# Transformer trunk on one Trainium2 core: one pool for the two MLP products, two pairs of the wide layer kept in DRAM as both parts, the fourth bank's seed put ahead

## The chip, the cores and the metric

The kernel runs on one core of one Trainium2 chip. TensorE (PE) multiplies matrices into PSUM banks, VectorE (DVE) and ScalarE (ACT) move and combine tiles, and SyncE (SP) does nothing but issue DMAs, one after the other, on one queue that 16 DMA engines serve. The metric is the device time of one execution in microseconds (us); a smaller one is better. Times in the text are counted from the start of the profiled span.

## The reference

One layer of a hybrid trunk over 2048 tokens of width 1024, all float32. A normalised input is projected once; some columns go through a short gated convolution, others through a chunked state-space scan; one output projection joins them, then comes the MLP, on which most of the change lies, and a last normalisation:

```python
h = rmsnorm(x, norm_mix_w)
proj = h @ w_in                              # 1024 columns to 5648
y_a = u_b * causal_dwconv(u_c * u_h, conv_w)
y_b = rmsnorm(ssd_scan(silu(conv(xbc)), dt, ...) * silu(z), norm_w)
x = x + concat(y_a, y_b) @ w_out
h = rmsnorm(x, norm_mlp_w)
hid = square(relu(h @ w_up))                 # 2048 x 4096: the wide layer
x = x + hid @ w_down
return rmsnorm(x, final_norm_w)
```

## The kernel before

**Number format.** Every large product is computed from two parts: a tile is cast to the type fp32r (the part `hi`, on ScalarE), and VectorE subtracts that from the tile (the part `lo`). Three matmuls make one product, `hi·hi`, `hi·lo`, `lo·hi` (lines 276 to 278, all of 128x512). Weights are split in the same way (lines 100 and 101: `whi`, `wlo`).

**Seven products.** A block of the MLP is cut 2 by 2 and computed by seven products in place of eight: b11, t1, t2, b21, t3, b22, t4, in this order, on combined operands. They add into the PSUM tiles px, py and pw. Right after b11, ScalarE copies px into a bank of its own, pw (line 283, the "seed"), on which b21 goes on. `chain` is the function that issues the seven, and after each it calls the code that empties the banks.

**Stages.** The up product runs in two halves of the tokens, each over 16 pairs of column blocks, 84 matmuls a pair; its input lies in four "places" u0 to u3 in SBUF, each with two parts (`uh`, `ul`). The result of a pair, after relu and square, is combined to seven blocks and stored to DRAM (`hid_d`, line 861 for three stores of two blocks, 862 for the seventh). The down product then reads the pairs back: `refill` loads them into raw tiles `rh` (line 970), and `settle` splits these into the places with a cast on ScalarE (347) and a subtraction on VectorE (348), which need the places to be free of the up product. `STEPS` says what the down product does in turn: step 0 handles output block d=0 with pairs 0 to 3, step 1 block d=2 with pairs 0 and 1, and so on. VectorE adds each bank to an `acc` tile (line 1018) that was loaded with the residual (line 978). The turn from the up to the down product, at about 2000 us, is where all of this meets; the text calls it the turn.

**Order.** The code is recorded in program order with tile pools; a scheduler then places the instructions of each engine. A tile that takes over a buffer waits for whoever used it last. The up product's pool (tags `utmp`, 8 buffers, and `uhid`, 5) is closed before the down product's (tag `acc`, 18) opens in the same memory. SP issues DMAs in its order, and each of them waits for the DMA that stands eight places ahead of it on the queue, or thereabouts (eight counters are used in turn, `DMAHW0` to `DMAHW7`).

**The scan** runs beside the projections, in 32 chunks. In each, ScalarE computes decays (lines 1268 and 1269: eight relus, a table load and an exp on `dec`, which a DMA brought), and casts `xde` to `xtok` (line 1276) for the first matmul of the state (`st`, line 113).

Of the kernel before, what the change touches and what calls it, by code (L numbers as in the profile page):

```python
# [11 lines left out]
F32 = mybir.dt.float32  # L12
# [14 lines left out]
EPS = 1e-5  # L27
FF = 4096
# [11 lines left out]
def trunk(ctx: ExitStack, tc: tile.TileContext, x, w_in, w_dt, w_out, w_up, w_down, cvec, hrow, out):  # L40
# [24 lines left out]
    hid_d = [[dram.tile([P, 7, TB], F32, name=f"hid_d{h}_{q}") for q in range(NQ)] for h in range(2)]  # L65
    sums_d = {}
# [124 lines left out]
    class Seven:  # L191
# [19 lines left out]
        def sums(self, e0, e1, e2, t4):  # L211

            self.sub(e2[:, 0], e2[:, 1], e0[:, 1])
            self.sub(e0[:, 1], e0[:, 1], e0[:, 0])
            self.sub(e1[:, 0], e2[:, 1], e0[:, 1])
            self.sub(t4, e1[:, 1], e1[:, 0])

# [27 lines left out]
        def chain(self, groups, ws, ahead, evict, after):  # L245
# [18 lines left out]
            for name, wn, half, acc in PRODUCTS:  # L264
# [568 lines left out]
    class Mlp(Seven):  # L833
# [18 lines left out]
        def wide(self, name):  # L852
            return self.up.tile([P, 2, TB], F32, tag="uhid", name=name, bufs=5)

        def store(self, h, q, e0, e1, e2):
            t4 = self.tmp("t4")
            if h == 1 and q >= LAST:
                nc.sync.dma_start(b12_d[:, q - LAST], e0[:, 1])
            self.sums(e0, e1, e2, t4)
            for i, e in enumerate((e0, e1, e2)):  # L860
                nc.sync.dma_start(hid_d[h][q][:, 2 * i : 2 * i + 2], e)
            nc.sync.dma_start(hid_d[h][q][:, 6], t4)

        def pair(self, h, q, ws, ahead, after):

            e0, e1, e2 = (self.wide(n) for n in ("e0", "e1", "e2"))
            s = {}
# [5 lines left out]
            def add(o, pm, name):  # L873
                nc.vector.tensor_tensor(out=o, in0=pm, in1=s[name], op=ALU.add)
# [5 lines left out]
            def evict(name, gi, pm):  # L880
                if name == "b11":
                    if gi not in self.seeds:
                        copy(pm["x"], "s1")
                elif name == "t1":
                    copy(pm["y"], "s5")
                elif name == "t2":
                    copy(pm["x"], "s2")
                elif name == "b21":
                    if gi in self.seeds:
                        relu2(e0[:, 0], pm["w"])  # L890
                    else:
                        add(e0[:, 0], pm["w"], "s1")
                        relu2(e0[:, 0], e0[:, 0])
                elif name == "t3":
                    add(e2[:, 1], pm["x"], "s5")
                    relu2(e2[:, 1], e2[:, 1])
                elif name == "b22":
                    add(e0[:, 1], pm["y"], "s2")
                    relu2(e0[:, 1], e0[:, 1])
                else:  # L900
                    relu2(e1[:, 1], pm["x"])

            got = self.chain([self.places], ws, ahead, evict, after)
            self.store(h, q, e0, e1, e2)
# [54 lines left out]
        def refill(self, gs, name):  # L959

            i = {"t1": 0, "b21": 1, "b22": 2, "t4": 3}.get(name)
            if i is not None:
                self.settle([self.wides.setdefault(g, {}) for g in gs], i, self.got)
            i = {"b11": 0, "t1": 1, "b21": 2, "b22": 3}.get(name)
            if i is not None:
                n = 1 if i == 3 else 2
                self.got = []
                for g in gs:
# [12 lines left out]
        def down(self, stack, ws):  # L981
# [75 lines left out]
        def rest(self, ws):  # L1057
# [11 lines left out]
            sums = [self.dp.tile([P, TB], F32, tag="acc", name="facc", bufs=18) for _ in range(NBB)]  # L1069
# [34 lines left out]
        def norm_out(self, tiles, bb, ts, st, *sums):  # L1104
# [3 lines left out]
            r = st.spread()  # L1108
# [14 lines left out]
        def rstd(self, w=TB):  # L1123
            return Rstd(self.dp, lambda n: self.raw(n)[:, 0], D, w)

        def finish_first(self):

            for bb in range(NBB):
# [8 lines left out]
                acc = self.dp.tile([P, TB], F32, tag="facc", name="facc", bufs=1)  # L1137
# [43 lines left out]
    class Scan:  # L1181
# [63 lines left out]
        def front(self, n):  # L1245
# [23 lines left out]
            nc.scalar.activation(dec, dec, AF.Exp, scale=-1.0)  # L1269
            for j in range(4):  # L1270
                nc.scalar.mul(t["xd"][:, j], t["xd"][:, j], col(C_D, 4 * g + j))
            for k, by in (("xdt", "dt"), ("xde", "dend")):
                t[k] = self.tmp()
                nc.vector.tensor_tensor(out=byhead(t[k]), in0=byhead(xtok), in1=t[by], op=ALU.mult)
            hi, lo = t["parts"] = [a.bitcast(F32R) for a in (self.tile([512], "xtok", 1), self.tmp())]
            nc.scalar.copy(hi, t["xde"])
            yield
            nc.vector.tensor_tensor(out=lo, in0=t["xde"], in1=hi.bitcast(F32), op=ALU.subtract)
# [310 lines left out]
    mlp.down(c4, ws)  # L1589
# [57 lines left out]
```

## Time and profile before

| | |
|---|---|
| time, median of 3 runs | 2655.2 us (2654.55 to 2656.59) |
| the profiled execution's own time | 2651.32 us |
| its span in the trace | 2649.1 us |
| mean granted clock of TensorE | 0.995 of full speed |
| busy share of PE, DVE, ACT | 98%, 73%, 55% |
| share of the DMA engines' time | 61.4% |

The profiled execution took 2.2 us more than its span, and 3.9 us less than the median. TensorE is busy nearly all the time, so what can be won or lost shows as the places where it isn't.

### The profile page before, as it was taken

To read this page: it belongs to the slowest core of one execution; us is meant where nothing else is said; L and a number is where in the kernel's file an instruction comes from. 1 tells how busy PE (TensorE), PEld (TensorE's weight loads), DVE (VectorE), ACT (ScalarE), POOL (GpSimd) and SP (SyncE) were. 2 spreads that over 40 slices of the span, in tenths; PEclk is the share of its full clock that TensorE was granted. 3 is DMA by queue.
4 is the path that set the end of the run, shared out by engine and by line. 5 is a ranking of instruction groups with operands and counts; after the bars stand their busy time and mean duration, and the time that the engine had idled before them with its cause. 6 is when DMAs were issued, how large, how long until landed. Compare 5 with 4: busy or idle time off the path is not lost.

```text
span 2649.1 us, 33645 instructions
## 1 busy us (share of the span) xinstructions
PE 2597.8 (98%) x12056; PEld 2133.7 (81%) x12056; DVE 1926.7 (73%) x2652; ACT 1455.0 (55%) x2212; POOL 54.0 (2%) x98
## 2 busy tenths in 40 slices
PE   7999999999999999999999999999999999999998
PEld 5788888788878888877888888888887888888887
DVE  7977867777778767767677775744447877888885
ACT  6654345776667666857336555755555444444543
POOL 0010000000000000000000000000000000000001
PEclk9999999999999999999999999999999999999999
DMA  3545745555555588877656786765558544665762
GB/s 145 197 175 187 274 143 200 185 161 171 175 163 165 163 272 258 265 205 220 202 203 230 258 314 238 273 216 192 197 194 290 155 151 150 217 205 176 244 207 69
DMA packets 292871, 536.96 MB, mean 203 GB/s; under 512 B 26208, under 2 KB 141920, under 8 KB 292704
## 3 DMA queue, kind: packets, MB, share of 16 engines
q1 hardware_dynamic: 292704, 534.82, 61.4%
q8 instruction: 94, 1.54, 0.2%
q14 instruction: 73, 0.60, 0.1%
HBM read 354.89 MB, written 179.83 MB: 202 GB/s over the span
## 4 chain that ended last, share of the span: by engine, by line
PE 61%; issue 25%; DMA 6%; ACT 5%; DVE 2%; SPq 0%; POOL 0%; POOLq 0%; DVEq 0%; ACTq 0%
PE px L276 9%; PE px L277 9%; PE px L278 9%; PE py L276 4%; PE py L278 4%; PE py L277 4%; PE pm L113 3%; PE pm L114 3%; PE pm L115 3%; DMA dec<-rd_d 3%; PE pw L276 2%; PE pw L278 2%; PE pw L277 2%; ACT dec L1268 1%; PE yd L1296 1%
## 5 line engine op out<-in xcount | busy, mean ns | idle before, releaser
L276 PE MATMUL px<-uh,whi 128*128 128x512 f32 x1672 | 656.5, 393 | 6.2 <-DVE acc L1018 2.0
L278 PE MATMUL px<-uh,wlo 128*128 128x512 f32 x1672 | 651.9, 390 | 0.0
L277 PE MATMUL px<-ul,whi 128*128 128x512 f32 x1672 | 651.5, 390 | 0.0
L276 PEld LDWEIGHTS px<-uh,whi 128*128 128x128 f32 x1672 | 314.2, 188 | 79.8 <-ACT s L727 3.6
L101 DVE TENSOR_TENSOR wlo<-wraw,whi 128x1024 fp32r<-128x1024 f32 x214 | 222.7, 1040 | 206.8 <-ACT whi L100 206.8
L278 PEld LDWEIGHTS px<-uh,wlo 128*128 128x128 f32 x1672 | 314.2, 188 | 66.2 <-issue 0.2
L277 PEld LDWEIGHTS px<-ul,whi 128*128 128x128 f32 x1672 | 314.4, 188 | 64.2
L100 ACT CAST whi<-wraw 128x1024 fp32r<-128x1024 f32 x214 | 193.9, 906 | 307.8 <-PE px L277 216.1
L100 ACT CAST whi<-s 128x1024 fp32r<-128x1024 f32 x210 | 219.8, 1047 | 227.8 <-PE py L277 98.1
L276 PE MATMUL py<-uh,whi 128*128 128x512 f32 x836 | 327.8, 392 | 5.4 <-DVE acc L1018 4.3
L277 PE MATMUL py<-ul,whi 128*128 128x512 f32 x836 | 325.9, 390 | 0.0
L278 PE MATMUL py<-uh,wlo 128*128 128x512 f32 x836 | 325.7, 390 | 0.0
L101 DVE TENSOR_TENSOR wlo<-s,whi 128x1024 fp32r<-128x1024 f32 x210 | 255.3, 1216 | 75.8 <-ACT whi L100 74.2
L113 PE MATMUL pm<-uh,whi 128*128 128x512 f32 (+1 forms) x648 | 251.7, 390 | 2.1 <-ACT uh L205 2.1
L114 PE MATMUL pm<-ul,whi 128*128 128x512 f32 (+1 forms) x648 | 248.6, 384 | 0.0
L115 PE MATMUL pm<-uh,wlo 128*128 128x512 f32 (+1 forms) x648 | 248.4, 383 | 0.0
L276 PEld LDWEIGHTS py<-uh,whi 128*128 128x128 f32 x836 | 157.2, 188 | 40.5 <-DVE acc L1018 4.8
L278 PEld LDWEIGHTS py<-uh,wlo 128*128 128x128 f32 x836 | 157.1, 188 | 32.9 <-DVE wlo L101 0.2
L277 PEld LDWEIGHTS py<-ul,whi 128*128 128x128 f32 x836 | 157.1, 188 | 32.0
L347 ACT CAST uh<-rh 128x1024 fp32r<-128x1024 f32 (+1 forms) x128 | 120.4, 944 | 80.7 <-PE py L278 62.7
L276 PE MATMUL pw<-uh,whi 128*128 128x512 f32 x418 | 163.3, 391 | 0.7 <-ACT pw L283 0.7
L278 PE MATMUL pw<-uh,wlo 128*128 128x512 f32 x418 | 162.9, 390 | 0.0
(239 smaller groups left out, 3777.1 us busy)
## 6 DMA issues: line engine op xcount, KB each, us to landing
hid_d<-e SPq DMA_DIRECT2D x96, 512.0 KB, 3.9
rh<-hid_d SPq DMA_DIRECT2D x96, 512.0 KB, 4.2
wraw<-w_in SPq DMA_DIRECT2D x68, 512.0 KB, 4.0
wraw<-w_down SPq DMA_DIRECT2D x104, 256.0 KB, 3.6
wraw<-w_up SPq DMA_DIRECT2D x48, 512.0 KB, 4.3
dec<-rd_d SPq DMA_DIRECT2D x32, 512.0 KB, 5.7
wraw<-w_out SPq DMA_DIRECT2D x32, 512.0 KB, 4.9
x_d<-xt SPq DMA_DIRECT2D x64, 256.0 KB, 3.5
```

The source lines that it names most:

```text
L100: nc.scalar.copy(hi, raw)
L101: eng.tensor_tensor(out=lo, in0=raw, in1=hi.bitcast(F32), op=ALU.subtract)
L113: nc.tensor.matmul(out, whi, hi, start=(k == 0), stop=False)
L114: nc.tensor.matmul(out, whi, lo, start=False, stop=False)
L115: nc.tensor.matmul(out, wlo, hi, start=False, stop=(k == nk - 1))
L276: nc.tensor.matmul(p, hi, h[0], start=not seeded and k == 0, stop=False, **kw)
L277: nc.tensor.matmul(p, hi, h[1], start=False, stop=False, **kw)
L278: nc.tensor.matmul(p, lo, h[0], start=False, stop=(k == len(g) - 1), **kw)
L347: nc.scalar.copy(p[i][0], t)
L1268: nc.scalar.activation(dec[:, i], dec[:, i], AF.Relu, bias=t["a"][:, i : i + 1], scale=-1.0)
L1296: nc.tensor.matmul(yd[(i % 2) * 64 : (i % 2) * 64 + 64, (i // 2) * L : (i // 2 + 1) * L], byhead(t["xdt"])[:, i, :], t["dec"][:, i, :], st ...
```

## The change

1. The up and the down product share one pool. All tiles of one block (`tmp`) now have one tag, `acc`, with 18 buffers; the pair's wide tiles e0, e1, e2 are gone, each block is a tile of its own, and a pair is stored block by block (7 stores, line 862 of the changed kernel, for 4). The normalisation at the end spreads its result into a `facc` tile.
2. `PARTED`: pairs 2 and 3 of the first half are split when they are made (line 865 cast, 866 subtraction) and stored as both parts (`part_d`, 14 stores a pair, line 868); at the turn, DMAs bring the parts straight into the places (line 973), without raw tile, cast or subtraction.
3. The residual loads for step 0 and after come in the order d = 0, 2, 1, 3.
4. The seed copy is recorded with a raised priority (`FIRST`).
5. In the scan, `xde`, its cast and its subtraction are written ahead of the decays in the program.

```diff
+FIRST = 200
...
+    PARTED = (2, 3)
+    part_d = {q: dram.tile([P, 2, 7, TB], F32, name=f"part_d{q}") for q in PARTED}
...
-                        nc.scalar.copy(pm[gi]["w"], pm[gi]["x"])
+                        with tc.high_priority(offset=FIRST):
+                            nc.scalar.copy(pm[gi]["w"], pm[gi]["x"])
...
-            return self.up.tile([P, TB], F32, tag="utmp", name=name, bufs=8)
...
-            return self.up.tile([P, 2, TB], F32, tag="uhid", name=name, bufs=5)
...
+            return self.up.tile([P, TB], F32, tag="acc", name=name, bufs=18)
...
+        BLOCKS = ("b11", "t1", "t2", "b21", "t3", "b22", "t4")
...
+        def store(self, h, q, e):
...
+            for i, n in enumerate(self.BLOCKS):
+                if h or q not in PARTED:
+                    nc.sync.dma_start(hid_d[h][q][:, i], e[n])
+                    continue
+                hi, lo = (self.tmp(m).bitcast(F32R) for m in ("ph", "pl"))
+                nc.scalar.copy(hi, e[n])
+                nc.vector.tensor_tensor(out=lo, in0=e[n], in1=hi.bitcast(F32), op=ALU.subtract)
+                for part, t in enumerate((hi, lo)):
+                    nc.sync.dma_start(part_d[q][:, part, i], t.bitcast(F32))
...
         def refill(self, gs, name):
+            whole = [g for g in gs if g not in PARTED]
             i = {"t1": 0, "b21": 1, "b22": 2, "t4": 3}.get(name)
             if i is not None:
-                self.settle([self.wides.setdefault(g, {}) for g in gs], i, self.got)
+                n = 1 if i == 3 else 2
+                self.settle([self.wides.setdefault(g, {}) for g in whole], i, self.got)
+                for g in gs:
+                    if g in PARTED:
+                        place = self.wides.setdefault(g, {})[i] = self.place(i)
+                        for part, t in enumerate(place):
+                            nc.sync.dma_start(t.bitcast(F32), part_d[g][:, part, 2 * i : 2 * i + n])
...
-                t[n] = self.dp.tile([P, TB], F32, tag="acc", name="acc", bufs=18)
+                t[n] = self.tmp("acc")
...
-            self.dp = stack.enter_context(tc.tile_pool(name="dp", bufs=1, reuse_waits="tile"))
-            for d in range(4):
+            for d in (0, 2, 1, 3):
                 self.outs(0, d)
...
+            for k, by in (("xde", "dend"), ("xdt", "dt")):
+                t[k] = self.tmp()
+                nc.vector.tensor_tensor(out=byhead(t[k]), in0=byhead(xtok), in1=t[by], op=ALU.mult)
+            hi, lo = t["parts"] = [a.bitcast(F32R) for a in (self.tile([512], "xtok", 1), self.tmp())]
+            nc.scalar.copy(hi, t["xde"])
             dec = t["dec"]
```

**TensorE at the turn.** `px_16719` is pair 15's last product t4, `px_16991`, `py_17012` and `pw_17004` are step 0 of the down product, and `px_17113`, `pw_17120`, `py_17132` step 1. Before:

```order
L276 MATMUL px_16991<-uh0_16763,whi_16815 128x512
...
L276 MATMUL py_17012<-uh0_16763,whi_16822 128x512 [waits Activation_49]
L276 MATMUL px_16719<-uh3_14619,whi_16702 128x512 [waits DVE_49]
...
L277 MATMUL py_17012<-ul0_16764,whi_16822 128x512
...
L276 MATMUL px_16991<-uh1_16826,whi_16822 128x512 [waits Activation_49]
...
L276 MATMUL pw_17004<-uh1_16826,whi_16815 128x512
...
L276 MATMUL px_17113<-uh0_16763,whi_17052 128x512 [waits Activation_49]
...
L276 MATMUL pw_17120<-uh1_16826,whi_17052 128x512 [waits Activation_49]
...
L276 MATMUL py_17132<-uh0_16763,whi_17059 128x512 [waits Activation_49]
...
L276 MATMUL py_17012<-uh2_16887,whi_16883 128x512 [waits DVE_49]
```

Step 0's first product stands ahead of pair 15's t4, and step 1's first four (`px_17113`, `pw_17120`, `py_17132`, 24 rows in all) ahead of the rest of step 0. After, with `px_16974` for pair 15's t4, `px_17235`, `py_17256` and `pw_17248` for step 0 and `px_17357` for step 1:

```order
L274 MATMUL py_16999<-uh2_14751,wlo_16937 128x512
L272 MATMUL px_16974<-uh3_14782,whi_16955 128x512 [waits DVE_49]
...
L272 MATMUL px_17235<-uh0_17014,whi_17063 128x512
...
L272 MATMUL py_17256<-uh0_17014,whi_17070 128x512 [waits Activation_49]
...
L272 MATMUL px_17235<-uh1_17074,whi_17070 128x512 [waits Activation_49]
...
L272 MATMUL pw_17248<-uh1_17074,whi_17063 128x512
...
L272 MATMUL py_17256<-uh2_17133,whi_17129 128x512 [waits DVE_49]
L272 MATMUL px_17235<-uh2_17133,whi_17129 128x512 [waits DVE_49]
...
L272 MATMUL px_17357<-uh0_17014,whi_17296 128x512 [waits Activation_49]
```

Pair 15's t4 moved ahead of step 0 and step 1 behind all of it: the row that waits for VectorE's add stands 48 rows behind step 0's first, and step 1 begins 84 rows behind it.

**SyncE at the turn.** `hid_d1_15` is pair 15's store, `wraw_17123` belongs to the weights of step 2, and `acc_16959` is the first residual tile. Before:

```order
L861 DMA hid_d1_15_144<-e0_16716 128x1024 [waits DMAHW3_49,DVE_49]
L861 DMA hid_d1_15_144<-e1_16717 128x1024 [waits DMAHW4_49,DVE_49,Activation_49]
L862 DMA hid_d1_15_144<-t4_16945 128x512 [waits DMAHW5_49,DVE_49]
L953 DMA wraw_17122<-w_down 128x384 [waits DMAHW6_49]
L953 DMA wraw_17123<-w_down 128x128 [waits DMAHW7_49,DVE_49,Activation_49]
...
L953 DMA wraw_17123<-w_down 128x384 [waits DMAHW1_49]
L978 DMA acc_16959<-x1_d0_77 128x512 [waits DMAHW2_49]
L978 DMA acc_16961<-x1_d1_78 128x512 [waits DMAHW5_49,DMAHW3_49]
L978 DMA acc_16963<-x1_d1_78 128x512 [waits DMAHW4_49]
```

After; `uh2` and `ul2` are the places' parts, `wraw_17250` the weights of step 1:

```order
L973 DMA ul1_17087<-part_d3_146 128x1024 [waits DMAHW0_49]
L980 DMA rh_17090<-hid_d0_0_113 128x1024 [waits DMAHW1_49,DVE_49]
...
L853 DMA b12_d_147<-t1_17122 128x512 [waits DMAHW5_49,Activation_49]
L973 DMA uh2_17141<-part_d2_145 128x1024 [waits DMAHW6_49,PE_49]
L973 DMA ul2_17142<-part_d2_145 128x1024 [waits DMAHW7_49]
...
L862 DMA hid_d1_15_144<-b11_17060 128x512 [waits DMAHW6_49]
...
L862 DMA hid_d1_15_144<-t4_17191 128x512 [waits DMAHW4_49,DVE_49]
L988 DMA acc_17203<-x1_d0_77 128x512 [waits DMAHW5_49]
L988 DMA acc_17205<-x1_d1_78 128x512 [waits DMAHW6_49]
L988 DMA acc_17207<-x1_d1_78 128x512 [waits DMAHW7_49]
...
L956 DMA wraw_17250<-w_down 128x256 [waits DMAHW5_49]
```

Sixteen loads of parts (four for each of u0 to u3, of 512 KB for u0 to u2 and 256 KB for u3) came in, the raw loads of pairs 2 and 3 went, and the weights of steps 1 and 2 moved from ahead of the 16 residual loads to behind them.

**ScalarE at pair 2 of the first half.** `pw` is the seed, `s5` and `s2` are copies of banks. Before:

```order
L878 ACTIVATE e1_12439<-e1_12439 128x512 [waits Activation_49]
L283 COPY pw_12607<-px_12594 128x512 [waits PE_49]
L871 COPY s5_12628<-py_12615 128x512 [waits DMAHW6_49,PE_49]
L100 CAST whi_12663<-wraw_12609 128x1024 [waits DMAHW0_49,PE_49]
L871 COPY s2_12642<-px_12594 128x512 [waits PE_49]
```

After:

```order
L280 COPY pw_12659<-px_12646 128x512 [waits PE_49]
L865 CAST ph_12603<-b11_12517 128x512
L865 CAST ph_12609<-t1_12565 128x512 [waits DMAHW5_49,DVE_49]
L865 CAST ph_12615<-t2_12596 128x512 [waits DMAHW1_49,DVE_49]
...
L865 CAST ph_12639<-t4_12598 128x512 [waits DVE_49]
L876 COPY s5_12680<-py_12667 128x512 [waits DMAHW5_49,PE_49]
L876 COPY s2_12694<-px_12646 128x512 [waits DVE_49,PE_49]
L103 CAST whi_12716<-wraw_12661 128x1024 [waits DMAHW0_49]
```

Seven casts of the finished pair stand between the seed and the copy of the next bank.

## Rows read from the trace of the kernel before

**Rows 1.** Page, parts 1 and 3: busy us (share of span) xinstructions; DMA queue

```profile
PE 2597.8 (98%) x12056; PEld 2133.7 (81%) x12056; DVE 1926.7 (73%) x2652; ACT 1455.0 (55%) x2212; POOL 54.0 (2%) x98
...
q1 hardware_dynamic: 292704, 534.82, 61.4%
```

**Rows 2.** TensorE's waits over the span: us in total, times, longest us

```profile
PE st L113 <- ACT xtok L1276: 8.1, 3, 4.5
PE py L276 <- DVE acc L1018: 4.3, 1, 4.3
```

**Rows 3.** 50-us windows: busy us (instructions) per engine, clock, DMA share, GB/s

```profile
1950.00:2000.00 50.00, 50.00 (x222) 41.40 (x221) 28.97 (x33) 31.89 (x45) 0.00 (x0) 1.00 0.66 230
2000.00:2050.00 50.00, 44.29 (x182) 35.19 (x181) 37.26 (x53) 21.13 (x32) 0.00 (x0) 0.93 0.85 288
2050.00:2100.00 50.00, 48.78 (x215) 40.09 (x214) 42.45 (x55) 20.99 (x24) 0.00 (x0) 1.00 0.50 156
```

**Rows 4.** TensorE's timeline, 2002 to 2031 us: start, us, what, idle before

```profile
2002.38 0.39 PE L276 MATMUL py<-uh,whi 128*128 128x512 f32 x1
...
2015.54 0.50 PE L276 MATMUL pw<-uh,whi 128*128 128x512 f32 x1 [0.66 <-ACT pw L283]
...
2017.90 0.50 PE L276 MATMUL py<-uh,whi 128*128 128x512 f32 x1 [0.71 <-ACT whi L100]
...
2020.58 0.39 PE L278 MATMUL px<-uh,wlo 128*128 128x512 f32 x1
2025.31 0.79 PE L276 MATMUL py<-uh,whi 128*128 128x512 f32 x1 [4.34 <-DVE acc L1018]
...
2030.17 0.48 PE L277 MATMUL px<-ul,whi 128*128 128x512 f32 x1
```

**Rows 5.** SyncE's queue, 1986 to 2034 us: start, us, DMAs issued

```profile
2016.22 0.32 SPq L862 DMA_DIRECT2D hid_d<-t  x1
2016.59 2.41 SPq L953 DMA_DIRECT2D wraw<-w_down  x4
2019.05 10.18 SPq L978 DMA_DIRECT2D acc<-x_d  x16
```

**Rows 6.** VectorE's timeline, 2005 to 2027 us

```profile
2015.50 0.69 DVE L209 TENSOR_TENSOR t<-e 128x512 f32<-128x512 f32 x1
...
2024.56 0.69 DVE L1018 TENSOR_TENSOR acc<-py,acc 128x512 f32<-128x512 f32 x1 [1.44 <-DMA acc<-x_d]
```

**Rows 7.** 5-us windows at the turn, columns as in the group above

```profile
1990.00:1995.00 5.00, 5.00 (x24) 4.14 (x23) 5.00 (x7) 3.63 (x5) 0.00 (x0) 1.00 1.00 354
...
2005.00:2010.00 5.00, 5.00 (x24) 4.14 (x23) 4.66 (x6) 4.61 (x7) 0.00 (x0) 1.00 0.92 288
...
2025.00:2030.00 5.00, 4.69 (x11) 3.73 (x12) 0.91 (x2) 0.00 (x0) 0.00 (x0) 0.50 1.02 357
2030.00:2035.00 5.00, 5.00 (x22) 4.08 (x22) 2.85 (x5) 1.06 (x1) 0.00 (x0) 0.97 1.06 391
```

**Rows 8.** DMA issues, 1975 to 2040 us: count, KB each, median to landing

```profile
acc<-x_d SPq DMA_DIRECT2D x16, 256.0 KB, 5.5
```

**Rows 9.** ScalarE's timeline before the second of the three scan waits

```profile
1156.81 1.57 ACT L1268 ACTIVATE dec<-dec,dd 128x128 f32<-128x128 f32 x5 [8.83 <-DMA dec<-rd_d]
...
1163.87 0.60 ACT L1276 CAST xtok<-stmp 128x512 fp32r<-128x512 f32 x1
```

**Rows 10.** TensorE's timeline at the second and the third scan wait

```profile
1164.52 0.50 PE L113 MATMUL st<-xtok,btok 128*128 128x512 f32 x1 [2.53 <-ACT xtok L1276]
...
1225.61 0.79 PE L113 MATMUL st<-xtok,btok 128*128 128x512 f32 x1 [4.47 <-ACT xtok L1276]
...
1227.36 1.91 PE L1293 MATMUL yo<-bc,state 128*128 128x128 f32 x8
```

**Rows 11.** ScalarE's timeline around pair 2 of the first half

```profile
1474.10 0.59 ACT L871 COPY s<-py 128x512 f32<-128x512 f32 x1 [2.15 <-PE py L278]
```

**Rows 12.** VectorE's timeline around pair 2 of the first half

```profile
1477.68 1.22 DVE L101 TENSOR_TENSOR wlo<-wraw,whi 128x1024 fp32r<-128x1024 f32 x1 [4.75 <-ACT whi L100]
```

More of the change, by code (lines that the diff above doesn't have):

```diff
@@ L849, in tmp @@
         def tmp(self, name):
[L850 to L862 removed]
+            return self.up.tile([P, TB], F32, tag="acc", name=name, bufs=18)
+        BLOCKS = ("b11", "t1", "t2", "b21", "t3", "b22", "t4")
+        def store(self, h, q, e):
+            if h == 1 and q >= LAST:
+                nc.sync.dma_start(b12_d[:, q - LAST], e["t1"])
+            for n in ("t2", "t3", "t4"):
+                e[n] = self.tmp(n)
+            self.sub(e["t3"], e["b22"], e["t1"])
+            self.sub(e["t1"], e["t1"], e["b11"])
+            self.sub(e["t2"], e["b22"], e["t1"])
+            self.sub(e["t4"], e["b21"], e["t2"])
+            for i, n in enumerate(self.BLOCKS):
[7 more added lines that the diff above has]
+                    nc.sync.dma_start(part_d[q][:, part, i], t.bitcast(F32))
         def pair(self, h, q, ws, ahead, after):
[L866 to L867 removed]
+            s, e = {}, {}
             def copy(pm, name):
@@ L873, in add @@
             def add(o, pm, name):
-                nc.vector.tensor_tensor(out=o, in0=pm, in1=s[name], op=ALU.add)
+                e[o] = self.tmp(o)
+                nc.vector.tensor_tensor(out=e[o], in0=pm, in1=s[name], op=ALU.add)
+                relu2(e[o], e[o])
             def relu2(o, i):
@@ L887, in evict @@
                     copy(pm["x"], "s2")
[L888 to L893, printed above, removed]
                 elif name == "t3":
-                    add(e2[:, 1], pm["x"], "s5")
-                    relu2(e2[:, 1], e2[:, 1])
+                    add("b22", pm["x"], "s5")
                 elif name == "b22":
[L898 to L901, printed above, removed]
+                    add("t1", pm["y"], "s2")
+                elif name == "b21" and gi not in self.seeds:
+                    add("b11", pm["w"], "s1")
+                elif name in ("b21", "t4"):
+                    o = "b11" if name == "b21" else "b21"
+                    e[o] = self.tmp(o)
+                    relu2(e[o], pm["w" if name == "b21" else "x"])
             got = self.chain([self.places], ws, ahead, evict, after)
-            self.store(h, q, e0, e1, e2)
+            self.store(h, q, e)
             return got
@@ L967, in refill @@
                 self.got = []
-                for g in gs:
+                for g in whole:
                     t = self.raw("rh")[:, 0:n]
@@ L1068, in rest @@
                     tiles[d + i, bb] = self.acc[1, d][n]
-            sums = [self.dp.tile([P, TB], F32, tag="acc", name="facc", bufs=18) for _ in range(NBB)]
+            sums = [self.tmp("facc") for _ in range(NBB)]
             for bb, t0, w in ((0, 0, TB), (1, 0, TB // 2), (1, TB // 2, TB // 2)):
@@ L1123, in rstd @@
         def rstd(self, w=TB):
-            return Rstd(self.dp, lambda n: self.raw(n)[:, 0], D, w)
+            return Rstd(self.up, lambda n: self.raw(n)[:, 0], D, w)
         def finish_first(self):
@@ L1135, in load @@
                     return t
-                acc = self.dp.tile([P, TB], F32, tag="facc", name="facc", bufs=1)
+                acc = self.facc()
                 for d in range(0, KD, 2):
@@ L1269, in front @@
             nc.scalar.activation(dec, dec, AF.Exp, scale=-1.0)
+            nc.vector.tensor_tensor(out=lo, in0=t["xde"], in1=hi.bitcast(F32), op=ALU.subtract)
+            yield
             for j in range(4):
                 nc.scalar.mul(t["xd"][:, j], t["xd"][:, j], col(C_D, 4 * g + j))
[L1272 to L1278, printed above, removed]
             nc.vector.tensor_tensor(out=dec, in0=dec, in1=sm.unsqueeze(1).to_broadcast([P, HG, L]), op=ALU.mult)
@@ L1588, in trunk @@
         ws = mlp.half(1, ws, iter(()))
-    mlp.down(c4, ws)
+        mlp.down(ws)
 def _lay_out(inputs):
```

9 lines of the change are left out of this document (2 added, 7 removed).

## The prediction

> **What bounds the kernel now.** I read the page's shares first: TensorE is busy 98% of the span, VectorE 73%, the DMA queue's engines 61% [rows 1]. So TensorE bounds the whole, and an edit elsewhere pays only where TensorE stands still. Second the waits of TensorE, to find those places. Two groups lie where the change reaches: the scan's state matmul, 8.1 us in three waits for a cast, and one of 4.3 us for VectorE's add to a residual tile [rows 2]. Third the 50-us windows, for what a place costs in all, the slow stretch behind a wait included. An undisturbed window has 222 matmuls, one per 50/222 = 0.225 us. The window from 2000 has 182 and the next 215, so the turn loses (40 + 7) × 0.225 = **10.6 us** [rows 3]. That is the prize.
>
> Its make-up is on the timeline: 0.66 us for the seed, 0.71 for a weight cast, and 4.34 at 2025.31; then eleven matmuls take 4.86 us (to 2030.17) for the 2.5 they need, 2.4 us lost, with the granted clock at 0.50 in that window, the lower of its two levels [rows 4, 7]. The rest is smaller gaps and what the second window loses.
>
> What is late for the 4.34? Backwards: the matmul waits for VectorE's add, whose start at 2024.56 waited for the DMA of the residual tile; that load stands in the group of 16 from 2019.05 on, behind pair 15's last store at 2016.22 and four weight loads; and that store waited for the block t4, which VectorE subtracted only at 2015.50 [rows 5, 6]. The residual tiles lie in memory that the pair's tiles must leave.
>
> **The change, part by part.**
>
> *Scan order.* The written order puts the cast ahead of the eight relus, but the order of ScalarE's rows in the second half of the scan is the same as before for chunks 19 to 31, the three waiting ones among them. There ScalarE waited 8.83 us for the decays' DMA and the cast came only after the relus and the exp, 7 us later [rows 9]; nothing of that moves. Cost 0; bound on the gain in the rivals.
>
> *Pairs 2 and 3, when they are made.* Seven casts of 0.59 us (a copy of that size on ScalarE) and seven subtractions of 0.69 a pair, 4.1 and 4.8 us. VectorE stands idle 4.75 us there, ScalarE 2.15 just before `s5` [rows 6, 11, 12]. The seven casts stand ahead of the `s5` copy and make it about 2 us late; TensorE needs that bank (py) again only at b22, three products (8 us) on. So 0. With that cover gone it would be 2 us a pair, 4 in all. The 14 stores are 3.7 MB for 1.8, 5 us more of the DMA engines' time a pair; the weights behind them are for the pair after next. The 18 tiles taken over belong to the pair before, whose stores stand ahead on the queue.
>
> *Settling at the turn.* Eight of 16 settles go from both engines, and t4 now stands ahead of step 0. In the new order t4 ends at 2002.38, where before step 0's first product ended [rows 4], so with relu and square at about 0.6 us each and a subtraction of 0.69 [rows 6, 11] its block is there by 2005, where its store was issued at 2016.22. This takes away the cause found above. The seed's wait (0.66) should go too.
>
> *Residual loads and parts, the term that decides.* Step 0 begins at 2002.38 and runs four products, 48 matmuls, to 2002.4 + 48 × 0.225 = 2013.2. Then it waits for residual tiles c22 and c12. Before, 24 matmuls of step 1 stood ahead of that wait; now none. So **break-even** is a resume at 2025.31 − 24 × 0.225 = 2019.9, not at 2025.31.
>
> When do the tiles land? All DMAs are on one queue in order. The first part loads wait for u0 to be free: t1 of pair 15 ends five products, 60 matmuls, before 2002.38, at 1988.9. From there to c12 the order holds: eight loads of 0.52 MB for u0 and u1 (4.2), raw loads of pairs 0 and 1 (1.57), b12 (0.26), u2 (2.1), u3 (1.05), seven stores of pair 15 (1.84), three residual tiles (0.79): 11.8 MB. Where the queue isn't held up, the engines move 357 to 391 GB/s at full share [rows 7]; mean 374, so 11.8/0.374 = 31.6 us, to 2020.5. The add and the restart took 0.75 us (2024.56 to 2025.31) [rows 4, 6]: **resume at 2021.3**, 1.4 us behind break-even. A second bound is latency: seven stores and three tiles at 0.64 us each (10.18/16 [rows 5]) from 2005 on are issued by 2011.4 and land 5.5 us later [rows 8]: 2016.9, resume 2017.7. I take the bytes, because the share is already 0.92 to 1.00 in this stretch before the change [rows 7] and the change adds 3.7 MB to it. A slow bound is 288 GB/s, which the window from 2005 shows with loads and stores mixed: 41 us, resume 2030.6.
>
> The Trainium skill (DMA: Bandwidth & Descriptors, "Where 436 GB/s comes from") gives about 358 GB/s as what HBM lets one core have; an estimate by that figure is 33 us and a resume at 2022.6. The trace differs: 391 GB/s in one window [rows 7].
>
> Then the lower clock again: 2.4 us. Step 1 begins 36 matmuls after the resume, at 2021.3 + 8.1 + 2.4 = 2031.8. Its weights now stand behind 13 more residual tiles: 3.9 MB with their own, 10.5 us after c12, at 2031.0; cast and subtraction of the first 128x512 take 0.59 + 0.69 us [rows 6, 11], to 2032.3. Wait 0.5 us.
>
> *Pool sharing at the end, the order d = 0, 2, 1, 3.* The first gives a tile that has long been free; the second brings step 1's tiles forward and is in the count. 0.
>
> **Sum.** Lost at the turn after: 2021.3 − 2013.2 = 8.1, plus 2.4, plus 0.5 = 11.0 us, against 10.6: +0.4. On the profiled execution's own time (2651.3, its span of 2649.1 and 2.2 around it) this is 2651.7; the median of the runs is 3.9 us above that execution, so 2655.6 as a median. I give 2655.5: no change. A measurement of this kernel can tell about 0.2%, 5.3 us.
>
> **Rivals.**
>
> *A. The tiles come by latency, the wait is short (faster).* For it: the stated cause does go, and the wait of 2.53 us in the scan was followed by no slow clock while one of 4.47 was: the eight matmuls behind it took 1.91 us [rows 10]. If the tiles land by 2015.5, the stall is 3.0 us and nothing else: 10.6 − 3.0 = 7.6 us gained, 2647.6. Latency alone (2017.7: 4.5 + 2.4 = 6.9) gives only −3.7. Against it: 11.8 MB by 2015.5 would be 444 GB/s, above every window. Chance 0.17.
>
> *B. The scan's waits go after all (faster).* 8.1 us of waits and about 3 us of low clock behind the longest: −11, 2644. Against it the unchanged rows. Chance 0.08.
>
> *C. The DMA engines become the bound at the turn (slower).* At 313 GB/s, between the mixed windows and the pure loads, 11.8 MB take 37.7 us: resume 2027.4, a stall of 14.2, 2.4 of clock and 2.6 for step 1's weights (12.6 us after c12, and 1.3): 19.2 lost, +8.6, 2663.8. It decides from a rate below about 335 GB/s, where the loss passes 5.3. For it: 288 GB/s is what the window from 2005 and the 50 us from 2000 moved [rows 3, 7]; against it, SyncE's queue was held up by VectorE in both. Chance 0.22.
>
> *D. The casts and the 14 stores of pairs 2 and 3 stall the up product (slower).* 2 to 3 us a pair, +5.5: 2660.7. Against it the idle time above, which holds all but 2 us of them. Chance 0.06.
>
> **How the numbers follow.** No change: 0.47, with its own range 2651 to 2660. Faster 0.17 + 0.08 plus 0.03 from the likeliest's own lower edge = 0.28. Slower 0.22 + 0.06 = 0.28, less 0.01 of D that stays under 5.3 = 0.27. Same 0.45. The range that leaves out less than 2 in 10 reaches into A and C but not to their ends: 2647 to 2663.
>
> **What would show it.** In the changed trace: t4 before step 0, and pair 15's last store near 2006 to 2013 (right), or still at 2016 (the pool wasn't the cause). The DMA share at 1.0 from 1989 to 2031 without a dip (the bytes bound), or dips there (latency, or SyncE waits for something else). One wait of TensorE in step 0 of 7 to 9 us, releaser VectorE's add, itself released by a residual DMA, followed by one low-clock window. Three scan waits of 8 us in sum, unchanged. The windows from 1450 to 1550 still at 222 matmuls. The prediction is wrong if the resume comes before 2016 or after 2026, if part loads are issued well after 1989, or if the scan's waits move.

## The result

| | median | runs | lowest to highest |
|---|---|---|---|
| before | 2654.69 us | 6 | 2650.77 to 2656.59 |
| after | 2661.12 us | 6 | 2657.08 to 2668.57 |

The change made the kernel slower: the ratio is 1.0040, with a 95% interval of 1.0027 to 1.0052. (The ratio is estimated over runs and is not the quotient of the two medians, which is 1.0024.) The profiled execution of the changed kernel took 2660.45 us with a span of 2658.2, 9.1 more than the span before. The forecast was no change, at 2655.5: the measured median lies inside its range of 2647 to 2663, but a loss clear of the scatter was not forecast.

### The profile page after: what moved, and what is told of

Read it like the earlier page. It is cut to its first block, busy times and chain, and to the rows that moved or that the text cites. A ratio compares the mean times of both kernels' runs of the same rounds, so it can differ in the third digit from the quotient of the medians.

```text
span 2658.2 us, 33813 instructions
## 1 busy us (share of the span) xinstructions
PE 2599.0 (98%) x12056; PEld 2133.8 (80%) x12056; DVE 1930.5 (73%) x2658; ACT 1455.8 (55%) x2218; POOL 55.4 (2%) x98
## 4 chain that ended last, share of the span: by engine, by line
PE 61%; issue 25%; DMA 6%; ACT 4%; DVE 3%; SPq 1%; POOL 0%; POOLq 0%; DVEq 0%; ACTq 0%
PE px L272 9%; PE px L273 9%; PE px L274 9%; PE py L272 4%; PE py L273 4%; PE py L274 4%; PE pm L116 4%; PE pm L117 4%; PE pm L118 4%; PE pw L272 2%; PE pw L273 2%; PE pw L274 2%; DMA dec<-rd_d 2%; PE yd L1305 1%; PE yo L1302 1%
## 5 line engine op out<-in xcount | busy, mean ns | idle before, releaser
L272 PE MATMUL px<-uh,whi 128*128 128x512 f32 x1672 | 657.0, 393 | 10.6 <-DVE acc L1027 4.2
L273 PE MATMUL pw<-ul,whi 128*128 128x512 f32 x418 | 162.6, 389 | 0.0
```

The source lines that it names most:

```text
L272: nc.tensor.matmul(p, hi, h[0], start=not seeded and k == 0, stop=False, **kw)
L273: nc.tensor.matmul(p, hi, h[1], start=False, stop=False, **kw)
```

## The profile after

TensorE's waits over the whole span come first, as in [rows 2]: us in total, times, longest. After, and the two groups of before that [rows 2] leaves out:

```profile
PE py L272 <- DVE acc L1027: 8.6, 1, 8.6
PE st L116 <- ACT xtok L1279: 7.5, 4, 3.5
PE px L272 <- DVE acc L1027: 4.2, 6, 1.5
PE px L272 <- ACT s L876: 2.8, 2, 1.7
```

```profile
PE px L276 <- DVE acc L1018: 2.0, 4, 1.2
PE px L276 <- ACT s L871: 0.8, 1, 0.8
```

The wait for the residual tile doubled, from 4.3 to 8.6 us. The scan's wait stayed. Two groups grew by about 2 us each: waits of px for VectorE's add, and those for `s`, the copy that ScalarE makes of a finished bank.

The 50-us windows answer to [rows 3] (columns as there); the first is the half turn of the up product, which was not looked at before.

```profile
1700.00:1750.00 50.00, 48.27 (x214) 39.65 (x213) 26.63 (x33) 29.45 (x46) 0.00 (x0) 1.00 0.82 278
1950.00:2000.00 50.00, 50.00 (x223) 41.40 (x222) 27.07 (x31) 28.96 (x42) 0.00 (x0) 1.00 0.71 239
2000.00:2050.00 50.00, 40.22 (x166) 31.43 (x165) 27.24 (x40) 16.36 (x24) 0.00 (x0) 0.93 0.93 342
2050.00:2100.00 50.00, 48.90 (x217) 40.20 (x216) 41.78 (x55) 20.10 (x22) 0.00 (x0) 1.00 0.52 159
```

From 2000 on 166 and 217 matmuls ran, 56 + 5 fewer than 222 each: 61 × 0.225 = 13.7 us lost at the turn, where 10.6 were lost before. The window from 1700 lacks 8, or 1.8 us; the same window before has 221.

TensorE's timeline at the turn (start, us, what, idle before it) answers to [rows 4]:

```profile
2003.36 0.39 PE L272 MATMUL px<-uh,whi 128*128 128x512 f32 x1
...
2014.02 0.39 PE L274 MATMUL pw<-uh,wlo 128*128 128x512 f32 x1
2023.02 0.80 PE L272 MATMUL py<-uh,whi 128*128 128x512 f32 x1 [8.62 <-DVE acc L1027]
...
2034.47 0.50 PE L274 MATMUL px<-uh,wlo 128*128 128x512 f32 x1 [0.51 <-DVE wlo L104]
...
2036.18 0.50 PE L272 MATMUL py<-uh,whi 128*128 128x512 f32 x1 [0.52 <-ACT whi L103]
```

Step 0 starts at 2003.36, runs its 48 matmuls without a gap, and then TensorE stands still until 2023.02. VectorE's timeline says for what ([rows 6]):

```profile
2007.99 2.43 DVE L345 TENSOR_TENSOR ul<-rh,uh 128x1024 fp32r<-128x1024 f32 x3 [0.24 <-ACT uh L344]
2010.34 0.69 DVE L212 TENSOR_TENSOR t<-t,b 128x512 f32<-128x512 f32 x1
2011.06 1.42 DVE L212 TENSOR_TENSOR t<-b,t 128x512 f32<-128x512 f32 x2
2021.68 0.69 DVE L1027 TENSOR_TENSOR acc<-pw,acc 128x512 f32<-128x512 f32 x1 [9.20 <-DMA acc<-x_d]
2022.29 0.68 DVE L1027 TENSOR_TENSOR acc<-py,acc 128x512 f32<-128x512 f32 x1
```

VectorE came to pair 15's last three subtractions only behind the settles of the raw pairs, finished them at 2012.5 and then waited 9.20 us for the DMA of a residual tile. Its add for py, which TensorE waits for, starts at 2022.29; before, it started at 2024.56 [rows 6]. So the tile is not later than before but 2.3 us earlier: the wait is longer because TensorE comes to it sooner, without step 1's 24 matmuls (5.4 us) and the waits of before ahead of it. SyncE's queue shows when that DMA was issued ([rows 5]):

```profile
1989.28 0.76 SPq L973 DMA_DIRECT2D uh<-part_d  x1
...
2008.63 0.32 SPq L973 DMA_DIRECT2D ul<-part_d  x1
2009.88 0.32 SPq L862 DMA_DIRECT2D hid_d<-b  x1
...
2016.20 0.32 SPq L862 DMA_DIRECT2D hid_d<-t  x1
2016.58 10.01 SPq L988 DMA_DIRECT2D acc<-x_d  x16
2026.94 5.12 SPq L956 DMA_DIRECT2D wraw<-w_down  x8
```

The first part load went out at 1989.28, pair 15's last store at 2016.20, the tiles from 2016.58 on. Were the DMA engines busy all that time, or was SyncE kept waiting? The 5-us windows answer ([rows 7]; the last three columns are the clock, the DMA share and GB/s):

```profile
1995.00:2000.00 5.00, 5.00 (x24) 4.14 (x23) 4.18 (x5) 3.60 (x6) 0.00 (x0) 1.00 1.02 383
...
2005.00:2010.00 5.00, 5.00 (x24) 4.14 (x23) 3.23 (x4) 3.67 (x6) 0.00 (x0) 1.00 1.04 415
...
2015.00:2020.00 5.00, 0.00 (x0) 0.00 (x0) 0.00 (x0) 0.00 (x0) 0.00 (x0) 0.94 1.05 403
2020.00:2025.00 5.00, 1.98 (x4) 1.44 (x5) 1.92 (x3) 0.00 (x0) 0.00 (x0) 0.50 1.03 386
2025.00:2030.00 5.00, 5.00 (x21) 4.00 (x21) 0.69 (x1) 0.00 (x0) 0.00 (x0) 0.88 1.05 390
```

The share stays full, without the dip of [rows 7], and 403 GB/s flow from 2015 to 2020, while all compute engines stand still. SyncE was held by the same engines: each of pair 15's seven stores waited last for a part load to land (4.7 us in all). The granted clock is down to 0.50 from 2020 to 2025, still within the wait for the most part.

A second difference is at the half turn, about 1709 us. ScalarE's timeline, after:

```profile
1705.97 0.58 ACT L876 COPY s<-py 128x512 f32<-128x512 f32 x1
1708.31 0.62 ACT L344 CAST uh<-rb 128x512 fp32r<-128x512 f32 x1 [1.75 <-DMA rb<-hn_d]
1708.83 0.58 ACT L876 COPY s<-px 128x512 f32<-128x512 f32 x1
```

and before:

```profile
1708.05 0.58 ACT L871 COPY s<-px 128x512 f32<-128x512 f32 x1
1708.53 0.61 ACT L877 ACTIVATE e<-pw 128x512 f32<-128x512 f32 x1
1709.18 0.62 ACT L347 CAST uh<-rb 128x512 fp32r<-128x512 f32 x1
```

In the changed kernel's order the copy of px stands behind a cast (for the second half's tokens) that waits 1.75 us for a DMA; before, the copy stood ahead of that cast. TensorE's timeline has the price:

```profile
1709.46 0.50 PE L272 MATMUL px<-uh,whi 128*128 128x512 f32 x1 [1.73 <-ACT s L876]
```

Both traces have 12056 matmuls, so a stretch can be measured from the n-th matmul's start to the m-th's. In us against the kernel before; "steps" are the later steps of the down product. The first row of numbers is what the stretch takes before.

| kernel | to no. 7800 | half turn, to 8000 | turn, 9150 to 9620 | steps, to 11850 | turn's acc wait of py |
|---|---|---|---|---|---|
| before | 1664.2 | 45.7 | 117.1 | 508.3 | 4.3 |
| after | −0.4 | +1.7 | +3.8 | +4.6 | 8.6 |
| e1_again | +0.4 | +1.5 | +5.2 | +1.5 | 9.0 |
| e2_no_parts | −1.7 | +1.5 | −0.4 | +1.8 | 0.6 |
| e3_seed_plain | −3.4 | +2.3 | +4.6 | +3.5 | 8.9 |
| e4_order_0123 | −3.3 | +2.3 | +4.9 | +5.0 | 8.6 |
| e5_early_residual | +2.7 | +1.8 | −0.4 | +1.1 | none |
| e6_early_no_parts | −2.8 | +1.6 | −1.7 | −1.1 | none |
| e7_one_pair | −1.5 | +1.1 | +6.8 | +1.5 | 10.3 |
| e8_three_pairs | +2.6 | +1.5 | +10.9 | +1.5 | 14.7 |
| e9_scan_before | −1.3 | +2.1 | +5.9 | +1.1 | 9.3 |
| e10_copies_first | −4.2 | +0.1 | +4.9 | +3.4 | 9.3 |
| e11_early_copies | −0.2 | +0.7 | −1.2 | +0.3 | none |
| e12_early_copies_scan | +6.3 | +0.7 | −0.6 | +1.8 | none |

From no. 8000 to 9150 every trace takes 260.7 us, 0.2267 a matmul, so 470 undisturbed ones would take 106.5: the turn loses 10.6 us before and 14.4 after. Each row is one execution. The first column and the last stretch move by several us with no pattern; the half turn and the turn repeat from kernel to kernel.

## The experiments

The theory to test (bytes): the parts put so much on the DMA engines between 1989 and 2022 that the residual tiles land late. Its rivals: the stores' chain (SyncE waits for something other than the engines), or one of the small edits. Diffs are against the changed kernel; ratios are against the kernel before.

**e1_again.** The changed kernel once more, for the scatter.

> The changed kernel itself, a second trace, to tell what repeats from what differs by chance. Against the kernel before, the first trace of the change lost 3.5 us at the turn to the down product, 1.7 us at the turn between the halves (TensorE waiting 1.73 us for ScalarE's copy s2, which stands behind a cast that waits for a DMA), and 4.9 us in small waits for VectorE's add between 2090 and 2560 us. Theory 'order and bytes': all three are set by the order of rows and the bytes on the queue, so they come back: 8.6 us (8 to 9.2) in step 0, 1.7 (1 to 2.5) between the halves, 3 to 6 in the later steps. Rival 'chance': the later steps' 4.9 us is the spread of one execution, and comes back as anything from 0 to 5; the two single waits change by more than 1 us. Time: ratio 1.003 to 1.005 to before either way.

1.0044 [1.0028, 1.0060]. The turn's wait and the half turn's came back (table); the +4.6 in the later steps did not, as the rival said of it.

**e2_no_parts.** All raw loads as before, the rest of the change kept.

```diff
-    PARTED = (2, 3)
+    PARTED = ()
```

> The change with no pair stored as parts; pairs 2 and 3 go through raw tile, cast and subtraction as before, everything else stays. Theory 'bytes': the wait of 8.6 us in step 0 is the time that 3.7 MB more take ahead of the residual tiles at about 395 GB/s (9.3 us), so it shrinks to 0 to 3 us; with step 1's first products again ahead of it the turn loses 4 to 8 us in all, 3 to 7 less than before the change's 10.6. Rival 'latency and issue': the residual tiles are late because pair 15's stores, each waiting for the DMA eight places ahead, hold the queue; then the wait stays at 4 us or more and the turn loses 10 or more. Time: 2651 to 2656 by bytes, 2655 to 2662 by the rival.

1.0005 [0.9994, 1.0017]: the loss is gone. TensorE's waits from 1985 to 2110:

```profile
PE px L272 <- DVE acc L1027: 3.2, 2, 2.9
...
PE py L272 <- DVE acc L1027: 0.6, 1, 0.6
```

The first line's 2.9 us lies near 2058, well behind step 0, where VectorE has no idle time ahead of its add. The turn was expected to lose 4 to 8 us and lost 10.2 (10.6 − 0.4): that part missed. So the parts make the kernel slow, not the shared pool, the seed or the order of the residual loads by themselves. But without parts step 1's first products stand ahead of step 0's wait again, so the time does not tell bytes from TensorE's order. VectorE's timeline and TensorE's say more:

```profile
2022.23 0.69 DVE L1027 TENSOR_TENSOR acc<-py,acc 128x512 f32<-128x512 f32 x1 [1.80 <-DMA acc<-x_d]
```

```profile
2022.98 0.50 PE L272 MATMUL py<-uh,whi 128*128 128x512 f32 x1 [0.65 <-DVE acc L1027]
```

The add for py starts at 2022.23 and step 0 goes on at 2022.98, in the changed kernel at 2022.29 and 2023.02. With or without parts the tile comes at the same time; the parts' bytes only take the place of the settling that holds SyncE here (it waits for `ul`, the settles' result, 9.1 us in nine from 1990 to 2022). The 8.6 us differ from 0.65 by what TensorE has to do ahead of the wait. That the row order alone makes the loss was not tested: no run changes that order and nothing else. Nor does the turn explain all: it gives back 5.2 + 0.4 = 5.6 us, and the medians (2664.31 and 2653.35) differ by 11.0.

**e3_seed_plain.** The seed copy without the raised priority.

```diff
-                        with tc.high_priority(offset=FIRST):
-                            nc.scalar.copy(pm[gi]["w"], pm[gi]["x"])
+                        nc.scalar.copy(pm[gi]["w"], pm[gi]["x"])
```

> The change with the seed copy at its ordinary priority. At the down product's turn SyncE's and TensorE's rows are the same as with the change, so both theories expect 8 to 9.2 us of wait there. Between the halves the copy s2 still stands behind the last two casts of the raw blocks on ScalarE, but the load for the last of them is one row earlier on SyncE. Theory 'the raised seed costs the 1.7 us': the wait there goes to 0 to 0.4. Rival 'the seven stores and the new order of casts cost it': it stays at 1 us or more. Seed waits elsewhere: at most 0.7 us in all. Time: within 2 us of the change.

1.0048 [1.0035, 1.0062]. The half turn's wait became 2.3 us for the seed itself, instead of for `s`: the raised seed is not what costs the 1.7 us.

**e4_order_0123.** The residual loads in the order of before.

```diff
-            for d in (0, 2, 1, 3):
+            for d in range(4):
```

> The change with the residual loads in the order d = 0, 1, 2, 3. Step 0's wait stays at 8 to 9.2 us (its four tiles are first in both). Theory 'order of the tiles': step 1 (d = 2) now finds its tiles four loads (1 MB, 2.7 us) later, which is still ahead of its weights, so nothing is lost there; and in the later steps the tiles of the second half take over buffers of outputs that ended one step earlier, so TensorE's wait of 0.7 us near 2315 goes and the later steps lose 1 us less. Rival 'the later steps lose by the late weights or by chance': the wait near 2315 stays. Time: within 2 us of the change.

1.0037 [1.0024, 1.0050], the wait 8.6 as with the other order: no part in it. The wait near 2315, which was to go, stayed (1.15 us), and the later steps lost as much as after (+5.0): the order of the tiles is not their cause.

**e5_early_residual.** Step 0's four residual tiles are asked for when pair 15 begins (they go out at 1991.87, ahead of every part load), the others step by step; the parts stay.

```diff
+                if last and h == 1:
+                    self.acc = {}
+                    self.outs(0, 0)
...
-            self.acc = {}
-            for d in (0, 2, 1, 3):
-                self.outs(0, d)
```

> The change with step 0's four residual tiles asked for ahead of pair 15's end (they then stand ahead of the part loads on SyncE's queue), step 1's four at step 0 and the other eight behind step 1's weights. The parts stay, and with them the bytes. Theory 'bytes': the wait of 8.6 us in step 0 goes to 0 to 1 us, and the queue's backlog shows at the next thing that is behind it: step 1's weights stand behind 13.6 MB from 1989 on, at 395 GB/s landing near 2024, against a need at 2021.4, so TensorE waits 2 to 5 us there, and the turn loses 4 to 8 us in place of 13 to 14. Rival 'it is the residual load alone (its latency, its place)': no wait above 1 us is left at the turn, which loses 0 to 3. Time: 2651 to 2656 by bytes, 2646 to 2651 by the rival.

1.0016 [1.0004, 1.0027]. The wait in step 0 is gone, but another came for step 1's weights (TensorE's timeline, ScalarE's, then two 5-us windows):

```profile
2031.14 0.79 PE L272 MATMUL px<-uh,whi 128*128 128x512 f32 x1 [4.96 <-ACT whi L103]
```

```profile
2030.47 0.62 ACT L103 CAST whi<-wraw 128x512 fp32r<-128x512 f32 x1 [16.12 <-DMA wraw<-w_down]
```

```profile
2015.00:2020.00 5.00, 5.00 (x24) 4.14 (x23) 4.96 (x8) 0.00 (x0) 0.00 (x0) 1.00 1.03 401
...
2025.00:2030.00 5.00, 1.18 (x6) 0.64 (x4) 0.69 (x1) 0.00 (x0) 0.00 (x0) 0.89 1.06 378
```

The engines are as full as ever, and the weights behind the parts are now what is late. A late transfer put ahead makes the next one late: with the engines full, that is what a backlog of bytes does. The wait of 5.0 us is in the range forecast, the turn's loss is not: 10.2 us for 4 to 8, about that of before and 4.2 less than after.

**e6_early_no_parts.** e5's edit and `PARTED = ()` together.

> The same with no pair stored as parts, so 3.7 MB fewer on the queue at the turn. Theory 'bytes': about 10 MB from 1989 on are through by 2015, every wait of the turn goes below 1.5 us each and the turn loses 0 to 4 us, where before lost 10.6: 4 to 8 us faster at the turn, 2645 to 2651 us. Rival 'settling': with all 16 settles back on ScalarE and VectorE, the places of u2 and u3 or the adds come late and TensorE waits 3 us or more for them: the turn loses 5 to 9, 2650 to 2655.

1.0009 [0.9998, 1.0019]. The turn is 1.7 us better than before in its trace, for the 4 to 8 expected: it loses 8.9. What is left are two waits for VectorE's add (1.3 us at 2015.01, 2.9 at 2057.72) and one of 1.9 for step 1's weights. The adds don't wait for residual tiles: VectorE's timeline has no idle time just ahead of either, settles and subtractions stand there. That is the rival, settling (3 us or more, a loss of 5 to 9); the runs show no gain over the kernel before.

**e7_one_pair and e8_three_pairs.** The dose.

```diff
-    PARTED = (2, 3)
+    PARTED = (3,)
```

and `(1, 2, 3)` for e8.

> The change with pair 3 alone stored as parts: TensorE's rows at the turn are the same as with the change, and 1.8 MB fewer stand ahead of the residual tiles. Theory 'bytes': at 395 GB/s the wait in step 0 is 4.6 us shorter, 3.5 to 5 us instead of 8.6 to 9.0. Rival 'order and latency': it stays at 8 us or more, since the stores of pair 15 still stand one behind the other ahead of the tiles.

> The change with pairs 1, 2 and 3 stored as parts: the same order of TensorE's rows, and 2.1 MB more ahead of the residual tiles (13.9 MB for 11.8). Theory 'bytes': the wait in step 0 is 5.3 us longer, 13 to 15 us. Rival 'order and latency': 8 to 10 us.

Three pairs: 1.0059 [1.0043, 1.0075] and a wait of 14.7 us, the number of the bytes theory. But not all of it is bytes. VectorE's timeline, SyncE's queue and a 5-us window of e8:

```profile
2025.19 0.69 DVE L212 TENSOR_TENSOR t<-t,b 128x512 f32<-128x512 f32 x1 [16.61 <-DMA b_d<-t]
```

```profile
2019.25 0.32 SPq L853 DMA_DIRECT2D b_d<-t  x1
...
2025.91 1.84 SPq L862 DMA_DIRECT2D hid_d<-t  x3
```

```profile
2025.00:2030.00 5.00, 0.00 (x0) 0.00 (x0) 2.08 (x3) 0.00 (x0) 0.00 (x0) 0.50 0.82 267
```

The part loads hold the small store of b12 until 2019.25; VectorE, which overwrites that tile, waits for it until 2025.19, the last three stores wait for VectorE, and the share falls to 0.82. The bytes delay the store on which this chain hangs, but how much of the 14.7 us each takes was not separated.

One pair: 1.0032 [1.0021, 1.0042], and a wait of 10.3, more than with two. That was a miss. The 5-us windows of e7, SyncE's queue and VectorE's timeline:

```profile
2005.00:2010.00 5.00, 5.00 (x24) 4.14 (x23) 4.44 (x7) 4.59 (x9) 0.00 (x0) 1.00 0.67 225
...
2015.00:2020.00 5.00, 0.00 (x0) 0.00 (x0) 2.08 (x3) 0.00 (x0) 0.00 (x0) 0.84 0.62 234
```

```profile
1997.97 8.16 SPq L980 DMA_DIRECT2D rh<-hid_d  x4
...
2008.17 0.47 SPq L853 DMA_DIRECT2D b_d<-t  x1
...
2017.51 1.77 SPq L862 DMA_DIRECT2D hid_d<-t  x3
2019.34 9.10 SPq L988 DMA_DIRECT2D acc<-x_d  x16
```

```profile
2016.80 0.69 DVE L212 TENSOR_TENSOR t<-t,b 128x512 f32<-128x512 f32 x1 [6.21 <-DMA b_d<-t]
```

Here the DMA engines are not full. Four raw loads kept SyncE for 8.16 us, as raw tiles have to be settled first (SyncE's waits for `ul` come to 12.6 us in eight from 1990 to 2022). So the small store of b12 went out only at 2008.17; VectorE waited 6.21 us for it to finish; the last three stores of pair 15 followed at 2017.51 and the residual tiles at 2019.34. The turn has two limits of about the same length, bytes and this chain. With two pairs eight of the 16 settles go and the bytes come; with one, twelve settles stay and the chain decides. In e7 the order of TensorE's first rows of step 0 is that of the changed kernel, so the long wait there is not bytes but the order and the chain together.

**e9_scan_before.** The scan's lines in the order of before (`xde`, its cast and its subtraction behind the decays).

> The change with the scan's order as it was before; all else as with the change. In the six traces with the new scan order the stretch of the first scan chunks (461 to 673 us of before) took 0.9 to 3.1 us longer than in before, and the two after it 1.5 to 3.2 and 0 to 4.7 less. Theory 'the scan edit does this': all three stretches come back to within 1 us of before, and the time is within 2 us of the change's (the three nearly cancel). Rival 'chance, or the pool': they stay as in the change.

1.0045 [1.0032, 1.0058]: as e1. TensorE's wait for `xtok` was 6.2 us in four, for 7.5 in four after and 8.1 in three before. The first scan stretch (461 to 673 us of before) was still 1.6 us longer than in before, so it did not come back as the theory said. The scan edit has no effect that these runs can tell.

**e10_copies_first.** The bank copies with the seed's raised priority, in the changed kernel.

```diff
-                nc.scalar.copy(s[name], pm)
+                with tc.high_priority(offset=FIRST):
+                    nc.scalar.copy(s[name], pm)
```

(in both functions named `copy`)

> The change with the copies of the banks (s1, s2, s5) at the seed's raised priority; on ScalarE this puts the copy s2 ahead of the cast that waits for a DMA between the halves, and changes nothing else there. Theory 'the order of the copy and the cast': TensorE's wait of 1.1 to 2.3 us for s2 there goes to 0 to 0.3, and nothing takes its place. Rival 'the loads of the raw blocks are late, the copy is only where it shows': TensorE waits as long, now for the place that this cast fills. Turn to the down product: as with the change (8.6 to 9.0 us).

1.0026 [1.0014, 1.0038]. The window that lacked 8 matmuls has them again, but for two (before has 221), and TensorE has no wait of over 0.2 us from 1690 to 1735:

```profile
1700.00:1750.00 50.00, 49.90 (x220) 41.03 (x219) 25.27 (x33) 29.01 (x44) 0.00 (x0) 1.00 0.84 283
```

The half turn's 1.7 us were the copy's place; e11 and e12, with the same edit, lose 0.7 there in a wait for VectorE. The ratio fell by 0.18%, more than 1.7 us, and the intervals of e1 and e10 overlap: the trace settles this point, the times alone would not.

**e11_early_copies and e12_early_copies_scan.** e6 with e10's edit; e12 also with e9's.

> No pair stored as parts, step 0's residual tiles asked for early, copies of the banks first: the three cures together, with the scan's new order. Theory 'the losses add': 1.5 us less than the same kernel without the copies' priority, which was 1.0009 of before (0.9998 to 1.0019); so 1.000 to 1.0005, not clearly faster than before. Rival 'the new order of everything costs too': 1.001 or more.

> The same with the scan's order as it was before. If the scan edit gains (its later stretches took less), this is 1 to 3 us slower than the run with the new order, 1.0005 to 1.0015; if it loses (its first stretch took more), 1 to 3 us faster, 0.999 to 1.000, the first version faster than both.

e11: 1.0002 [0.9993, 1.0012]; e12: 1.0007 [0.9998, 1.0017]. With the parts gone, the residual tiles early and the copies ahead, the kernel is as fast as before. No version tried here beats it.

## Why the prediction missed

1. **Time and sign.** No change had the highest chance, 0.45; +0.4% is the case that was given 0.27. The working said 11.0 − 10.6 = +0.4 us at the turn and nothing elsewhere. The trace shows +3.8 at the turn (+3.1 by 50-us windows), +1.7 at the half turn, and a scatter in the rest. The runs lost more than these 5.5: about 10.6 us by the ratio, 6.4 by the medians.

2. **The wait at the turn was foreseen.** The wait was forecast at 8.1 us behind 48 matmuls of step 0, for VectorE's add, for a residual DMA, with the share at 1.0 throughout. It was 8.62, with all of that. Step 0 began 1.0 us later than thought (2003.36 for 2002.38) and the wait ended 1.7 later (2023.02 for 2021.3). Two mistakes in the bytes nearly cancelled: the engines moved more (the six windows from 1990 to 2020 average 392 GB/s, for the 374 taken), and had more to move: by those windows about 12.6 MB from 1989.28 to 2021.5, for the 11.8 counted. What was left out of the count is argued, not shown: the five stores issued just before 1989.28, still under way. The last 0.6 us is that pw's add stands ahead of py's. One step on the way was wrong without a price: pair 15's last block was forecast by 2005 and VectorE had it at 2012.5, behind the settles of the raw pairs; the stores waited for the full engines in any case.

3. **The step that failed is the subtraction.** The 10.6 us before came from the windows, which hold everything; the 11.0 after were three named terms. Of the 10.6, the terms 0.66, 0.71, 4.34 and 2.4 make 8.1; the other 2.5 were called "smaller gaps and what the second window loses" and had no counterpart on the other side. Counted from one matmul's start to the next, over the turn's stretch of the table (us lost; the sums are taken before rounding):

| | before | forecast after | after |
|---|---|---|---|
| waits for the seed and for weights | 1.9 | 0.5 | 2.0 |
| wait for the residual tile | 4.5 | 8.1 | 8.8 |
| low clock behind it | 2.5 | 2.4 | 1.7 |
| later wait for VectorE's add (near 2060 and 2065) | 1.5 | none | 1.3 |
| smaller gaps | 0.2 | none | 0.5 |
| sum | 10.6 | 11.0 | 14.4 |

The last two terms, put at nothing without a reason, stayed (1.9 us), and step 1's weights, forecast at 0.5 us, cost 2.0; the wait and the clock were 0.7 off each, in opposite directions. The prediction held a better number itself: a resume 1.4 us behind break-even and 0.5 for the weights make +1.9, where its sum said +0.4, and the two were not compared.

4. **"Costed at nothing" failed at the half turn.** The order of ScalarE's rows was read at pair 2 of the first half and at the turn only. At the half turn a bank copy had moved behind a cast that waits for a DMA: 1.1 to 2.3 us in every changed kernel up to e9, 0.1 in e10. This term was put at nothing without a reading.

5. **The stated tests.** Pair 15's last store came at 2016.20, not by 2013, although VectorE was done at 2012.5. The prediction would have read that as "the pool wasn't the cause". The store alone can't tell: VectorE was done 3.7 us earlier than before, and SyncE was held by the full engines instead. e2 bears the reading out: with the shared pool and all settles its last store goes out at 2017.34, no earlier than the 2016.22 of before. The resume, due between 2016 and 2026, was in bounds.

6. **What held.** The scan edit changed nothing in ScalarE's waits that could be told (8.1 to 7.5 us). The windows from 1450 to 1550 have 223 and 222 matmuls, so the casts and 14 stores a pair were hidden and rival D did not happen. The order d = 0, 2, 1, 3 was free (e4).

7. **The rivals.** C had the right place, sign and resource, but not its price: it needed under 335 GB/s, and the engines were faster than even the forecast had it. The Trainium skill (DMA: Bandwidth & Descriptors, "Where 436 GB/s comes from") gives about 358 GB/s as one core's share of HBM. The resume by that figure, 2022.6, comes nearest to 2023.02, but by accident: the windows above show up to 415 GB/s, and the measurement decides.

**Open.** About half of the loss is unexplained. The later steps of the down product took 4.6 us more in the profile after, 1.5 in e1, the same program. TensorE's waits for VectorE's add there were 3.1 us in five after, 0.8 in three before, 0.7 in three in e1. What sets them was not found. And 5.6 us at the turn do not account for the 11.0 between the medians of e1 and e2; the traced execution of e1 (2658.89 us) is the shortest of its five, and what the longer ones lost is in no trace.

## What to carry to other kernels

Price both sides of a change by the same view: a loss read from windows must not be set against a sum of named waits, or the unnamed rest looks like a gain. Work that is taken off ScalarE and VectorE and put on DMA engines that are already full in that stretch only changes which limit ends last: the add that TensorE waits for started at 2022.23 without the parts and at 2022.29 with them. Moving one transfer ahead on such a queue (e5) moves the wait to the next one, 5.0 us in place of 8.6. What stands ahead of a wait counts as much as the time of the tile: the same tile cost 0.65 us with step 1's products ahead and 8.6 without. Read the new order of every engine at every stage border, not only at the edit: one copy behind a cast that waits for a DMA cost 1.7 us far from any edited line.

## What the runs showed of the hardware

With parts loaded straight into place, the DMA engines held 383 to 417 GB/s in every 5-us window from 1995 to 2030, at a share of 1.02 to 1.05, loads and stores mixed, where a mixed window before had 288 [rows 7]; e5 shows 401 to 413 from 2000 to 2025. The 288 was no limit of the engines. The low clock behind TensorE's wait did not cost more for a longer wait. Counted from start to start it cost 1.7 us behind the wait of 8.62 and 2.7 behind that of 9.0 in e1, the same program; 2.9 behind 14.7 in e8, 1.7 to 2.9 in all eight traces with the wait in step 0; and 2.5 behind 4.34 before. Part of the low clock falls into the wait itself, where it costs nothing: in the changed kernel it was 0.50 from 2020 on, 3 us ahead of the resume.
